# Eight gate tiles as four Strassen pairs, with a rearranged head, LayerNorm and last product, in a decoder layer

## The chip, the cores and the metric

The kernel runs on one NeuronCore of a Trainium2 chip. The metric is the device time of one execution in microseconds (us). Before the change the median of three runs is 1666.04 us (1663.42 to 1666.61).

## The reference

One step of a one-layer decoder over 16 meta tokens, 1024 prompt tokens and 8 samples of 8 new tokens, all in fp32:

```
u = rmsnorm(h);  z = u @ w_in + b_in            # 1024 -> 6144 columns
a, c, q, k, v, g = split(z)                     # g: three gates of 1024 channels
y_a = causal pooling of a, linear map           # branch A
y_b = GLU(c) -> depthwise conv, width 31 -> LayerNorm -> silu -> w_co   # branch B
y_c = attention(q, k, v) @ w_ao                 # branch C
h  += (sig(g0)*y_a + sig(g1)*y_b + sig(g2)*y_c) @ w_out
h  += relu(rmsnorm(h) @ w_up)**2 @ w_down
y   = rmsnorm(h)
```

The prompt's attention looks back 128 positions; the samples attend to a cache. The states of pooling, convolution and attention are outputs too.

## The kernel before

Activations lie with channels on the 128 partitions and tokens along the row: T = 1104 with the meta tokens, L = 1088 without. Every fp32 product is made of three fp32r products: a value is split into a high half (a rounding copy on ScalarE) and a low half (the value minus the high half, on DVE), and `mm3` (line 145) adds hi·hi, hi·lo and lo·hi in PSUM. So each weight tile costs a DMA, a ScalarE copy and a DVE subtraction ahead of its matmuls; `Weights` (line 45) does this: `split_to` emits the copy, and the subtraction is queued later, by `flush` or, one or two chunks on, by `tick`.

The input projection (lines 1042 to 1134) is 48 tiles of 128 output channels in the order of `TILES` (line 28), each in three token chunks `CH` of 416, 320 and 368 columns (400 instead of 416 where meta tokens aren't needed), with 24 matmuls a chunk. The first five tiles are the head (lines 1042 to 1115): there the norm isn't known yet, so raw x times the norm's weight is multiplied (`head_split`), and `head_stats` (line 341) makes the squares, their sums over channels (a matmul against ones, line 242), the reciprocal root on DVE and ScalarE, and a broadcast back by matmul (line 253); `rb` holds it, and `proj_chunk` scales by it. The last 13 tiles are gate tiles (kind "z"): `proj_chunk` (line 877) evicts each chunk on ScalarE with the bias (line 916) and stores it to a DRAM buffer `gD`.

Between chunks `slot` (line 207) runs one item of `attq` and some of `dveq`. `attq` holds attention: two items a unit (`even`: scores, transposes of the unit before, exponentials; `odd`: product with values, the next unit's split of q, normalization), then the samples, then loads and splits of the attention output `Ox` (`tail_slices`), then LayerNorm (`ln_steps`, put in by `after_conv` once `dveq` is empty). `dveq` holds the convolution's 31 taps of four channel groups and the pooling sums, two DVE instructions an item. An item of `attq` can say how many of `dveq` go with it: 1 in attention and in the samples' last six steps, none in their first eight; without one it is two (`NDVE`). Each engine works in the order in which its instructions are emitted.

Then come the attention output projection with the pooling product (lines 1155 to 1178, `pool_out`), the convolution's output projection (1190 to 1207), w_out (1321 to 1407), the up stage (1566 to 1632) and the down stage (1749 to 1809). The up stage takes two output tiles at a time by Strassen's identity in Winograd's form: weights A and activations B are cut into 2 x 2 blocks (two tiles by two halves of channels, two halves of channels by two halves of tokens), and seven products of sums of blocks, each of 24 matmuls of 272 columns, take the place of eight. `sum_pair` makes sums of weight blocks, `prep` splits a product's weights three products ahead, `product` multiplies. The down stage does the same over whole products, with sums that went through DRAM. Its last product (n = 6, lines 1780 to 1807) goes through the tokens in two parts; `residual` (line 1673) loads the saved h and adds it, through `page2`, a pool of five buffers.

Large buffers are 40 pages of T columns (`page`, line 124). PSUM has eight banks: three "pm" and two "qk" for main products (the "qk" ones are in the rotation only while `wide` is set), three "px" for the rest.

Of the kernel before, what the change touches and what calls it, by code (L numbers as in the profile page):

```python
# [7 lines left out]
F32 = mybir.dt.float32  # L8
# [27 lines left out]
NHEAD = 5  # L36
LAST_A = max(i for i, t in enumerate(TILES) if t[0] in "ac")
NDVE = (2, 2)
SMP = [0] * 8 + [1] * 6

# [4 lines left out]
class Weights:  # L45
# [10 lines left out]
    def load_to(self, n):  # L56
        while self.nraw < min(n, len(self.jobs)):
            i = self.nraw
            src, w, paged = self.jobs[i]
            t = self.tile("wraw", F32, w, paged)  # L60
            self.nc.sync.dma_start(t, src)
            self.raw[i] = t
            self.nraw += 1

    def load_half(self, i, h):
        src = self.jobs[i][0]
        if h == 0:
            self.raw[i] = self.tile("wraw", F32, 1024, False)
            self.nraw = i + 1
        c = slice(512 * h, 512 * h + 512)  # L70
        self.nc.sync.dma_start(self.raw[i][:, c], src[:, c])

    def split_half(self, i, h):
        if h == 0:
            self.out[i] = [self.tile(t, F32R, 1024, False) for t in ("whi", "wlo")]
            self.nsplit = i + 1
        c = slice(512 * h, 512 * h + 512)
# [4 lines left out]
    def split_to(self, n):  # L82
        while self.nsplit < min(n, len(self.jobs)):
            i = self.nsplit
            self.load_to(i + 1)
            _, w, paged = self.jobs[i]
# [25 lines left out]
def hybrid_trunk_kernel(ctx, tc, I, O):  # L112
# [46 lines left out]
    jobs = [(I["w_in"][i], 1024, 1 < i < NHEAD) for i in range(48)]  # L159
    WAO = [48, 49] + list(range(51, 57))  # L160
    WPOOL = 50
    jobs += [(I["w_ao"][m], 1024, False) for m in range(8)]
# [6 lines left out]
    W = Weights(nc, pool, page, jobs)  # L169


    one = pool.tile([P, 4], F32, name="one", tag="st", bufs=8)
# [4 lines left out]
    def load_x(ci, k0=0, k1=8):  # L177
# [3 lines left out]
        for k in range(k0, k1, n):  # L181
            m = min(n, k1 - k)
            t = page("x")[:, :m * w].rearrange("p (k c) -> p k c", k=m)
# [4 lines left out]
    vec = const("vec", [P, NV])  # L188
    W.load_half(0, 0)
    load_x(0, 0, 4)  # L190
    W.load_half(0, 1)
    load_x(0, 4, 8)
    bin_ = const("b_in", [P, 48])
    W.load_half(1, 0)
    W.load_half(1, 1)
# [145 lines left out]
    def head_stats():  # L341
        x = X[0]
        sq = [t[:, o:o + b0] for t in [page("acc") for _ in range(3)] for o in (0, 512)]
        acc, sq = sq[:2], sq[2:]
# [9 lines left out]
        def s1():  # L354
            for i in range(3, 8):
                q = sq[1 + i % 3] if i > 3 else acc[1]
                A.activation(q, x[i], AF.Square)
# [1584 lines left out]
```

## Time and profile before

| | |
|---|---|
| median of three runs | 1666.04 us (1663.42 to 1666.61) |
| the profiled execution | 1661.65 us |
| its span on the core | 1659.8 us |
| mean granted TensorE clock | 0.997 of full speed |
| matmuls | 11552 |

In the profile PE is TensorE's matmuls, PEld its weight loads, DVE VectorE, ACT ScalarE, POOL GpSimd, SP SyncE, whose queue issues nearly all DMAs. A timeline row is start (us from the span's start), duration, engine, line, operation, output tile <- input tiles, shapes and count, and in brackets the idle time of the engine just before and what ended it. A matmul's duration includes its way through the array, so the rate is read from start to start. Where a row stands for several instructions, the duration is theirs together.

### The profile page before, as it was taken

Reading aid. Unit: us, or ns where it says so; the run is one execution under the profiler, and the core shown is the slowest. Engines: PE = TensorE matmul, PEld = TensorE weight load, DVE = VectorE, ACT = ScalarE, POOL = GpSimd, SP = SyncE. Lnnn points to the kernel's source line nnn. Section 1 sums busy time; section 2 is a strip of 40 time slices with the busy share of each in tenths; the row PEclk is TensorE's granted clock in tenths of the full one; section 3 lists DMA queues with packets and bytes.
Section 4 is the critical chain, followed back from the end, with each engine's and each line's share of the span. In section 5 each row is a group of like instructions: output and inputs, shape, how many; then the busy total and the mean of one; then the engine's idle time right before and its main releaser. Section 6 shows DMA issues by size and latency. Waiting matters only on the chain.

```text
span 1659.8 us, 29142 instructions
## 1 busy us (share of the span) xinstructions
PE 1637.1 (99%) x11552; PEld 1612.9 (97%) x11552; DVE 1111.1 (67%) x1877; ACT 748.2 (45%) x1424; POOL 314.4 (19%) x258
## 2 busy tenths in 40 slices
PE   8999999999999999999999999999999999999987
PEld 7999999999999999999999999999999999999987
DVE  7786767867667576344474688888887844466665
ACT  6537667467674342364243443332233533333331
POOL 1010000000010002212102535555555200000000
PEclk9999999999999999999999999999999999999999
DMA  6051221221225263353243357777776855566633
GB/s 207 15 122 39 83 67 44 72 70 51 71 69 174 97 207 102 106 210 119 93 163 134 132 165 252 242 245 246 247 244 230 324 191 183 183 198 200 209 134 102
DMA packets 132349, 250.78 MB, mean 151 GB/s; under 512 B 33428, under 2 KB 64629, under 8 KB 132213
## 3 DMA queue, kind: packets, MB, share of 16 engines
q1 hardware_dynamic: 131796, 248.53, 45.4%
q8 instruction: 90, 1.47, 0.4%
q14 instruction: 47, 0.38, 0.1%
q10 hardware_dynamic: 416, 0.39, 0.1%
HBM read 168.52 MB, written 80.36 MB: 150 GB/s over the span
## 4 chain that ended last, share of the span: by engine, by line
PE 94%; DVE 2%; DMA 1%; issue 1%; ACT 1%; SPq 0%; DVEq 0%; ACTq 0%
PE pm L148 13%; PE pm L150 13%; PE pm L149 13%; PE m L1652 7%; PE m L1648 7%; PE m L1650 7%; PE m L1458 6%; PE m L1456 6%; PE m L1459 6%; PE pn L148 3%; PE pn L149 3%; PE pn L150 3%; PE px L622 2%; PE px L610 2%; PE qk L569 2%
## 5 line engine op out<-in xcount | busy, mean ns | idle before, releaser
L148 PE MATMUL pm<-uh,whi 128*128 128x320 f32 (+3 forms) x1008 | 338.0, 335 | 6.4 <-ACT uh L324 6.4
L149 PE MATMUL pm<-ul,whi 128*128 128x320 f32 (+3 forms) x1008 | 332.2, 330 | 1.1 <-DVE ul L325 1.0
L150 PE MATMUL pm<-uh,wlo 128*128 128x320 f32 (+3 forms) x1008 | 331.8, 329 | 0.0
L1652 PE MATMUL m<-oph,wlo 128*128 128x272 f32 (+2 forms) x896 | 259.3, 289 | 3.1 <-DVE wlo L91 3.1
L1648 PE MATMUL m<-oph,whi 128*128 128x272 f32 (+2 forms) x896 | 259.5, 290 | 1.2 <-ACT whi L90 1.2
L1650 PE MATMUL m<-opl,whi 128*128 128x272 f32 (+2 forms) x896 | 258.9, 289 | 0.0
L90 ACT ACTIVATE whi<-wraw 128x1024 fp32r<-128x1024 f32 (+1 forms) x127 | 130.1, 1026 | 223.1 <-PE m L1650 145.1
L91 DVE TENSOR_TENSOR wlo<-wraw,whi 128x1024 fp32r<-128x1024 f32 (+1 forms) x127 | 157.8, 1244 | 88.1 <-ACT whi L90 88.0
L148 PEld LDWEIGHTS pm<-uh,whi 128*128 128x128 f32 x1008 | 190.2, 189 | 7.7 <-ACT uh L324 6.4
L149 PEld LDWEIGHTS pm<-ul,whi 128*128 128x128 f32 x1008 | 190.3, 189 | 3.7 <-DVE ul L325 3.1
L150 PEld LDWEIGHTS pm<-uh,wlo 128*128 128x128 f32 x1008 | 190.1, 189 | 0.1
L1652 PEld LDWEIGHTS m<-oph,wlo 128*128 128x128 f32 x896 | 169.4, 189 | 3.6 <-DVE wlo L91 3.6
L1648 PEld LDWEIGHTS m<-oph,whi 128*128 128x128 f32 x896 | 169.7, 189 | 1.4 <-ACT whi L90 1.4
L1650 PEld LDWEIGHTS m<-opl,whi 128*128 128x128 f32 x896 | 169.6, 189 | 0.0
L444 DVE SCALAR_TENSOR_TENSOR y<-ext,vec,y 128x1024 f32<-128x1024 f32 x120 | 154.7, 1289 | 0.0
L1456 PE MATMUL m<-bch,wlo 128*128 128x272 f32 x448 | 129.1, 288 | 0.6 <-DVE cb L1599 0.6
L1456 PE MATMUL m<-bch,whi 128*128 128x272 f32 x448 | 129.1, 288 | 0.2 <-ACT s L1591 0.2
L1459 PE MATMUL m<-bch,whi 128*128 128x272 f32 x448 | 129.1, 288 | 0.0
L1459 PE MATMUL m<-bch,wlo 128*128 128x272 f32 x448 | 129.1, 288 | 0.0
L1458 PE MATMUL m<-bcl,whi 128*128 128x272 f32 x448 | 129.0, 288 | 0.0
L1458 PE MATMUL m<-bcl,wlo 128*128 128x272 f32 x448 | 129.0, 288 | 0.0
L558 POOL TENSOR_TENSOR uq<-q,uq 128x128 fp32r<-128x128 f32 x64 | 34.7, 564 | 391.9 <-ACT uq L557 391.9
(373 smaller groups left out, 3725.2 us busy)
## 6 DMA issues: line engine op xcount, KB each, us to landing
wraw<-w_in SPq DMA_DIRECT2D x46, 512.0 KB, 3.8
opT<-d SPq DMA_DIRECT2D x64, 272.0 KB, 3.2
ld<-opT SPq DMA_DIRECT2D x32, 544.0 KB, 4.7
wd<-w_down SPq DMA_DIRECT2D x32, 512.0 KB, 6.2
sumD<-wd SPq DMA_DIRECT2D x32, 512.0 KB, 4.9
wraw<-sumD SPq DMA_DIRECT2D x32, 512.0 KB, 3.6
gt<-gD SPq DMA_DIRECT2D x24, 544.0 KB, 4.6
ld<-opB SPq DMA_DIRECT2D x23, 544.0 KB, 4.8
```

The source lines that it names most:

```text
L90: self.nc.scalar.activation(hi, r, AF.Copy)
L91: self.late.append(lambda lo=lo, r=r, hi=hi: self.nc.vector.tensor_tensor(lo, r, hi.bitcast(F32), ALU.subtract))
L148: PE.matmul(ps, lhsT=wh[k], rhs=xh, start=first and i == 0, stop=False)
L149: PE.matmul(ps, lhsT=wh[k], rhs=xl, start=False, stop=False)
L150: PE.matmul(ps, lhsT=wl[k], rhs=xh, start=False, stop=last and i == n - 1)
L444: V.scalar_tensor_tensor(y[:, :NP], e[:, k:k + NP], w, y[:, :NP], ALU.mult, ALU.add)
L1456: PE.matmul(ps, lhsT=wh, rhs=xh, start=first and k == 0, stop=False, skip_group_check=True)
L1458: PE.matmul(ps, lhsT=wh, rhs=xl, start=False, stop=False, skip_group_check=True)
L1459: PE.matmul(ps, lhsT=wl, rhs=xh, start=False, stop=k == 3, skip_group_check=True)
L1648: PE.matmul(ps, lhsT=wh[:, w], rhs=xh[:, r], start=k == 0, stop=False, skip_group_check=True)
L1650: PE.matmul(ps, lhsT=wh[:, w], rhs=xl[:, r], start=False, stop=False, skip_group_check=True)
L1652: PE.matmul(ps, lhsT=wl[:, w], rhs=xh[:, r], start=False, stop=k == 15, skip_group_check=True)
```

## The change

- **Gate tiles.** The plain loop ends after 40 tiles (`NZ`). The last eight, all gate tiles, are computed as four pairs with the up stage's seven products. Activations come from the split u: `z_sums` adds the halves back together and makes four sums, for each of four channel pairs, all on DVE, behind four chosen chunks of tiles 37 to 39; `z_split` splits the results T1 to T4. Tile 39 takes its chunks in the order 1, 2, 0. The attention buffers are given up before the first pair, and `page2` opens there. The first pair's sums of weights are made during and just behind tile 39, the next ones a pair ahead, on DVE.
- **Around them.** In attention's `odd` items two taps go instead of one; the last pooling group's steps go to the head of `dveq`. LayerNorm is queued after the pairs, in the attention output stage. `Ox` is loaded and split in the last pair. Sums of LayerNorm, the pooling product's add and the low half of q move from GpSimd to DVE.
- **Head.** The first loads are cut finer, x's first chunk has a layout of its own, `vec` is loaded by ScalarE's queue, 16 matmuls of zeros go ahead, all eight squares are made on ScalarE with seven adds on DVE. The matmuls that sum over tokens (hs[2]) now stand behind tile 2's first chunk, and tile 3's first chunk stands ahead of the broadcast (hs[3]).
- **Last product.** Residual loads are issued in products 3 to 5, in halves of `page2` buffers (`residual_load`); three weight tiles of the last product are loaded at the end of product 5, and two of its tiles are loaded into `page2`.

```diff
+NWARM = 16
+NZP = 4
+NZ = 48 - 2 * NZP
...
-    vec = const("vec", [P, NV])
-    W.load_half(0, 0)
-    load_x(0, 0, 4)
-    W.load_half(0, 1)
+    W.load_part(0, 0, 2)
+    load_x(0, 0, 2)
+    W.load_part(0, 2, 4)
+    load_x(0, 2, 4)
+    W.load_part(0, 4, 8)
     load_x(0, 4, 8)
...
     def head_stats():
...
-        def s0():
-            for i in range(3):
-                q = sq[0] if i else acc[0]
-                G.tensor_tensor(q, x[i], x[i], ALU.mult)
-                if i:
-                    G.tensor_tensor(acc[0], acc[0], q, ALU.add)
...
+        def s1(ks):
+            def go():
+                for i in ks:
+                    q = sq[i % 2] if i else acc
+                    A.activation(q, x[i], AF.Square)
+                    if i:
+                        V.tensor_tensor(acc, acc, q, ALU.add)
+            return go
...
-            G.tensor_tensor(acc[:, :L], Y[0][:, :L], Y[1][:, :L], ALU.add)
+            V.tensor_tensor(acc[:, :L], Y[0][:, :L], Y[1][:, :L], ALU.add)
...
-                G.tensor_tensor(self.ql[:, i], q, self.qh[:, i].bitcast(F32), ALU.subtract)
+                V.tensor_tensor(self.ql[:, i], q, self.qh[:, i].bitcast(F32), ALU.subtract)
...
-            out += [(even(n, not first), 1), (odd(n, not first), 1)]
+            out += [(even(n, not first), 1), (odd(n, not first), 2)]
...
+    def z_sums(k):
+        ua, ub = zt[k] = page("zu"), page("zu")
+        lo, hi = slice(0, HL), slice(HL, L)
+        for t, n in ((ua, k), (ub, k + 4)):
+            V.tensor_tensor(t[:, :L], Uh[n][:, NM:].bitcast(F32), Ul[n][:, NM:].bitcast(F32),
+                            ALU.add)
+        V.tensor_tensor(ua[:, lo], ua[:, hi], ua[:, lo], ALU.subtract)
+        V.tensor_tensor(ua[:, hi], ub[:, hi], ua[:, hi], ALU.subtract)
+        V.tensor_tensor(ub[:, hi], ub[:, hi], ua[:, lo], ALU.subtract)
+        V.tensor_tensor(ub[:, lo], ub[:, lo], ub[:, hi], ALU.subtract)
...
+    wz = paux()
+    for _ in range(NWARM):
+        PE.matmul(wz[:, :256], lhsT=warm[:, :P], rhs=warm[:, P:], start=True, stop=True)
...
-    hs[2]()
     proj_open(2)
     b0_.append(proj_mm(2, 0))
+    hs[2]()
     W.split_to(4)
     W.flush()
     for k in range(4, 8):
         head_split(1, k)
+    proj_open(3)
+    b0_.append(proj_mm(3, 0))
     hs[3]()
     W.split_to(5)
     W.flush()
...
-    proj_open(3)
-    b0_.append(proj_mm(3, 0))
     proj_chunk(1, 0, b0_[1])
...
+    ZS = [(NZ - 3, 2), (NZ - 2, 0), (NZ - 2, 2), (NZ - 1, 0)]
+    for ti in range(NHEAD, NZ):
         proj_open(ti)
         W.split_to(ti + 2)
+        if ti == NZ - 1:
+            load_pair(-NZP)
+        for n, ci in enumerate((0, 1, 2) if ti < NZ - 1 else (1, 2, 0)):
+            if ti == NZ - 1 and n:
+                sum_pair(-NZP, n - 1)
+            proj_chunk(ti, ci)
+            if (ti, n) in ZS:
+                z_sums(ZS.index((ti, n)))
+            if ti == NZ - 1 and n:
+                z_split("T2", 2 * n - 2)
+                z_split("T2", 2 * n - 1)
+                prep(-7 * NZP + n - 1)
+            slot(1, NDVE[0] if attq else NDVE[1])
+        proj_close(ti)
...
+    load_pair(1 - NZP)
+    for k in range(4):
+        z_split("T1", k)
+    prep(-7 * NZP + 2)
+    for n in (2, 3):
+        sum_pair(-NZP, n)
+    for x in ("T3", "T4"):
+        attq.extend(lambda x=x, k=k: [z_split(x, k), z_split(x, k + 1)] for k in (0, 2))
+    oq = [load_split(Ox, "o", oD[j]) for j in range(8)]
+    for s in range(-7 * NZP, 0):
+        j, i = divmod(s, 7)
...
+        if s + 3 < 0:
+            prep(s + 3)
+        if j < -1:
+            if 2 <= i < 6:
+                sum_pair(j + 1, i - 2)
...
+        product(b, s, i, i in (0, 1, 5), z_comb)
...
+        slot(1, 2)
+    dveq.append(after_conv)
+    wide.append(0)
...
-            G.tensor_tensor(pt[:, a:c], pt[:, a:c], g0[:, a:c], ALU.add)
+            V.tensor_tensor(pt[:, a:c], pt[:, a:c], g0[:, a:c], ALU.add)
...
+    def residual_load(m, half):
...
     def residual(m, half):
         a, c = half
-        t = page2("hr")
-        SP.dma_start(t[:, :HL], hD[m][:, a:c])
+        t = hr.pop((m, a))
...
+                if 3 <= n < 6 and hf:
+                    if n != 5:
+                        residual_load(2 * mp + (n == 3), HI)
+                    if n != 3:
+                        residual_load(2 * mp + (n == 5), LO)
+                if n == NPROD - 2 and q == 7:
+                    W.load_to(i + 4)
                 dprod(n, mp, hf, b, TWO)
                 WD.pop((n, mp, hf))
-                slot()
+                slot(3 if n == 4 and hf == 0 else 1)
```

## Rows read from the trace of the kernel before

**Rows 1.** The page's first part: busy time, share of the span, instructions.
```profile
PE 1637.1 (99%) x11552; PEld 1612.9 (97%) x11552; DVE 1111.1 (67%) x1877; ACT 748.2 (45%) x1424; POOL 314.4 (19%) x258
```

**Rows 2.** Waits of TensorE: line, who, us in total, times, longest.
```profile
PE m L1652 <- DVE wlo L91: 3.1, 2, 2.4
...
PE m L1648 <- ACT whi L90: 1.2, 1, 1.2
```

**Rows 3.** Timeline of ScalarE, 578 to 607 us: samples' last copy, evictions of chunk 2.
```profile
578.74 0.77 ACT L770 ACTIVATE os<-spv 64x256 f32<-64x256 f32 x2 [0.68 <-PE spv L765]
...
594.72 0.57 ACT L916 ACTIVATE zs<-pn,b_in 128x368 f32<-128x368 f32 x1 [3.49 <-PE pn L150]
...
606.56 0.57 ACT L916 ACTIVATE zs<-pm,b_in 128x368 f32<-128x368 f32 x1 [1.48 <-issue]
```

**Rows 4.** Timeline of ScalarE in the up stage: eviction of product 6, four pairs apart.
```profile
1005.18 0.62 ACT L1605 ACTIVATE cb<-m 128x544 f32<-128x544 f32 x1 [2.32 <-PE m L1459]
...
1089.26 0.62 ACT L1605 ACTIVATE cb<-m 128x544 f32<-128x544 f32 x1 [2.32 <-PE m L1459]
```

**Rows 5.** Timeline of DVE, 569 to 599 us.
```profile
569.01 1.23 DVE L91 TENSOR_TENSOR wlo<-wraw,whi 128x1024 fp32r<-128x1024 f32 x1 [4.86 <-ACT whi L90]
570.15 1.28 DVE L444 SCALAR_TENSOR_TENSOR y<-ext,vec,y 128x1024 f32<-128x1024 f32 x1
...
571.54 1.28 DVE L444 SCALAR_TENSOR_TENSOR y<-ext,vec,y 128x1024 f32<-128x1024 f32 x1
...
584.41 1.23 DVE L91 TENSOR_TENSOR wlo<-wraw,whi 128x1024 fp32r<-128x1024 f32 x1 [7.22 <-ACT whi L90]
...
596.32 2.50 DVE L154 TENSOR_TENSOR ol<-ld,oh 128x1088 fp32r<-128x1088 f32 x2 [7.89 <-ACT oh L153]
```

**Rows 6.** Timeline of DVE, 949 to 952 us: sums and splits of 544 columns.
```profile
949.01 0.72 DVE L1363 TENSOR_TENSOR t<-u 128x544 f32<-128x544 f32 x1
...
950.45 1.36 DVE L154 TENSOR_TENSOR bcl<-t,bch 128x544 fp32r<-128x544 f32 x2 [0.72 <-ACT bch L153]
```

**Rows 7.** Windows: length; busy PE, PEld, DVE, ACT, POOL; PEclk, DMA share, GB/s.
```profile
1599.60:1602.00 2.40, 0.08 (x1) 0.09 (x1) 2.37 (x4) 0.00 (x0) 0.00 (x0) 0.99 0.01 3
1602.00:1605.40 3.40, 3.40 (x14) 3.40 (x15) 1.85 (x7) 2.15 (x3) 0.00 (x0) 0.50 0.51 154
```

**Rows 8.** Timelines of the head: two rows of ScalarE, four of DVE, two of TensorE.
```profile
8.62 2.27 ACT L324 ACTIVATE uh<-x,vec 128x416 fp32r<-128x416 f32 x4
...
26.24 0.52 ACT L371 ACTIVATE rb<-px 128x416 f32<-128x416 f32 x1 [1.08 <-PE px L253]
...
12.29 2.32 DVE L325 SCALAR_TENSOR_TENSOR ul<-x,vec,uh 128x416 fp32r<-128x416 f32 x4
...
22.00 0.16 DVE L228 TENSOR_SCALAR st<-st 128x4 f32<-128x4 f32 x1
...
24.03 1.22 DVE L91 TENSOR_TENSOR wlo<-wraw,whi 128x1024 fp32r<-128x1024 f32 x1
...
27.74 1.23 DVE L91 TENSOR_TENSOR wlo<-wraw,whi 128x1024 fp32r<-128x1024 f32 x1 [0.64 <-ACT whi L90]
...
19.72 0.95 PE L242 MATMUL st<-ones,acc 128*128 128x1 f32 x8
...
34.95 0.72 PE L242 MATMUL st<-ones,sq 128*128 128x1 f32 x6
```

**Rows 9.** Timelines of the last product: DVE and TensorE.
```profile
1598.60 0.73 DVE L1678 TENSOR_TENSOR h<-h,hr 128x544 f32<-128x544 f32 x1 [5.56 <-DMA hr<-hD]
...
1601.92 0.60 PE L1652 MATMUL m<-oph,wlo 128*128 128x288 f32 x1 [2.37 <-DVE wlo L91]
```

**Rows 10.** Groups by form: a pooling product's eviction, busy us, mean ns, idle before.
```profile
L1150 DVE SCALAR_TENSOR_TENSOR gt<-pm,vec,gt 128x416 f32<-128x416 f32 x11 | 6.8, 647 | 0.6 <-ACT whi L90 0.4
```

**Rows 11.** Timelines of ScalarE and TensorE in attention, 142 to 147 us.
```profile
142.39 1.71 ACT L601 ACTIVATE lg<-lg,usm 128x256 f32<-128x256 f32 x4 [0.69 <-DVE usm L599]
...
145.52 1.09 PE L610 MATMUL px<-ident,lg 128*128 128x128 f32 x8
```

More of the change, by code (lines that the diff above doesn't have):

```diff
@@ L157, in hybrid_trunk_kernel @@
     ctx.enter_context(sched)
[L159 to L162, printed above, removed]
+    W = Weights(nc, pool, page, [(I["w_in"][i], 1024, 1 < i < NHEAD) for i in range(NZ)])
+    WAO = [0, 1] + list(range(3, 9))
+    WPOOL = 2
+    jobs = [(I["w_ao"][m], 1024, False) for m in range(8)]
     jobs.insert(WPOOL, (I["w_pool"], 1024, True))
@@ L168, in hybrid_trunk_kernel @@
     jobs += [(I["w_out"][m], 1024, False) for m in MORD]
-    W = Weights(nc, pool, page, jobs)
+    vec = pool.tile([P, NV], F32, name="vec", tag="vec")
+    A.dma_start(vec, I["vec"])
     one = pool.tile([P, 4], F32, name="one", tag="st", bufs=8)
@@ L475, in fin @@
             store(rD[g], r[:, :L])
[L476 removed]
+        fs = [add(n, 1 << n) for n in range(g + 1)] + [fin]
+        if g == 3:
+            dveq[:0] = fs
+        else:
+            dveq.extend(fs)
     Sx = []
@@ new lines, in prep @@
+    def prep(s):
+        j, i = divmod(s, 7)
+        a, b = raws[j]
+        x = ORD[i]
+        if x[0] == "A":
+            src = {"A11": a[:, :512], "A12": a[:, 512:], "A22": b[:, 512:]}[x]
+        else:
+            n = int(x[1]) - 1
+            src = Ssum[j][n // 2][:, 512 * (n % 2):512 * (n % 2) + 512]
+        tag = ("whi", "wlo")[s % 2]
+        t = pool.tile([P, 1024], F32R, name=tag, tag=tag, bufs=2)
+        split(t[:, :512], t[:, 512:], src)
+        WX[s] = t
+        if i == 6:
+            raws.pop(j)
+            Ssum.pop(j)
@@ new lines, in product @@
+    def product(b, s, i, first, op):
+        t = WX.pop(s)
+        for ch in range(2):
+            for k in range(4):
+                wh, wl = (t[:, o + 128 * k:o + 128 * k + 128] for o in (0, 512))
+                xh, xl = op(BX[i], k, ch)
+                ps = b[ch][:, :HL // 2]
+                PE.matmul(ps, lhsT=wh, rhs=xh, start=first and k == 0, stop=False,
+                          skip_group_check=True)
+                PE.matmul(ps, lhsT=wh, rhs=xl, start=False, stop=False, skip_group_check=True)
+                PE.matmul(ps, lhsT=wl, rhs=xh, start=False, stop=k == 3,
+                          skip_group_check=True)
@@ new lines, in hybrid_trunk_kernel @@
+    print("left", len(attq), len(dveq))
+    while attq:
+        slot(1, 1)
+    slot(0)
+    apool_ctx.__exit__(None, None, None)
+    pool2 = ctx.enter_context(tc.tile_pool(name="sb2", bufs=1, reuse_waits="tile"))
+    load_pair(1 - NZP)
+    for k in range(4):
+        z_split("T1", k)
[5 more added lines that the diff above has]
+    oq = [load_split(Ox, "o", oD[j]) for j in range(8)]
@@ new lines, in hybrid_trunk_kernel @@
+        if i > 4:
+            store(gD[TILES[ti + i - 5][1]], c[:, :L])
+        if i == 4 and j < -2:
+            load_pair(j + 2)
+        if j == -1:
+            if i == 4:
+                W = Weights(nc, pool, page, jobs)
+                W.load_to(2)
+                W.split_to(1)
+                W.flush()
+            for n in ((), (), (0, 1), (2, 3), (), (4, 5), (6, 7))[i]:
+                oq[n][1]()
+            for n in ((0, 1, 2), (), (3, 4), (5, 6), (7,), (), ())[i]:
+                oq[n][0]()
```

274 lines of the change are left out of this document (152 added, 122 removed).

## The prediction

> **What bounds the kernel now.** I read the page first: TensorE is busy for 99% of the span [rows 1], so time is either taken out of the matmul stream or put into gaps of it. TensorE's own list of waits came next [rows 2]: the last down product waits 3.1 us for a DVE split and 1.2 us for a ScalarE one, and in the rest of the kernel it hardly waits. Then the stages: ScalarE's evictions of the gate tiles give their period, since TensorE never pauses there: one tile (72 matmuls of 400, 320 and 368 columns) takes 606.56 - 594.72 = 11.84 us [rows 3], 164 ns a matmul. The up stage already runs the same identity on pairs with 272 columns a matmul: (1089.26 - 1005.18) / 4 = 21.02 us a pair [rows 4], 168 matmuls of 125 ns. Last, DVE around the place of the change: a tap costs 571.54 - 570.15 = 1.39 us, and DVE sits idle for 7.22 us before 584.41 [rows 5]: there is some room, and the question is how much.
>
> Durations are from the profiled execution, 1661.65 us (span 1659.8), 4.4 us under the median of 1666.04. The sum is made against 1661.65 and carried over to the median.
>
> **1. Matmuls of the eight tiles.** Two plain tiles take 23.68 us, a pair 21.02: 2.66 us saved on each of four pairs, -10.7 us. The fixed cost of a matmul eats half of the eighth that the identity saves. Product order, accumulators and evictions are the up stage's, which leaves TensorE without a wait, so inside the pairs I cost evictions, copies and pair sums (0.64 us on DVE each) at nothing: some 10 us of DVE work lie beside 21 us of matmuls. The Trainium skill speaks against this step (TensorE: Matmul & The Clock Gate, Back-to-back issue gap): it gives a sustained 81 ns for 128 columns and 131 ns for 512. A straight line through these is an estimate of 100 ns for 272 and 112 ns for the mean of 363, and a pair would be 0.7 us longer than two tiles, +2.8 us in all. The rows of this kernel have 125 and 164 ns and decide for the gain.
>
> **2. DVE at the first pair.** All new sums are queued on DVE, in order, behind taps. The rows give their prices: a low half of a weight 1.14 us to the next start, a tap 1.39, two 1088-wide ones 2.50 [rows 5], a 544-wide one 1.36 - 0.72 = 0.64 [rows 6], taken for 512 too. One z_sums is 2.50 + 4 x 0.64 = 5.06 us. Up to the low half at 569.01 the queue is unchanged in number, and DVE waits for that one, so this is where I start. From it to the low half of the first product's weights stand 2 low halves (2.3), 11 taps (15.3; counted from the slots, two each once attention is done), 4 z_sums (20.2), one pair sum, two T2 splits and the split itself (2.6): 40.4 us, so 609.4. Tile 39 ends on TensorE at 606.4 [rows 3]. The second product multiplies T1: before its splits come 3 more taps, one sum, two T2 splits and a weight split (6.7 us), then four T1 splits of 0.64: the first is done at 616.8, the last at 618.7. After that 14 of the 24 matmuls remain, 1.75 us: the second product ends at 620.4 where 606.4 + 6.0 = 612.4 was due, 8.0 us late. A gap of this size halves the clock: after the 2.4 us gap in the last product it was granted 0.50 for 3.4 us [rows 7], and part of that falls after the wait, 0.6 us. So +8.6 us. Bounds: 6 (splits and sums at 0.6, clock kept) and 16 (third rival).
>
> **3. Head.** Smaller first loads, 16 dummy matmuls and the squares moved off GpSimd bring the first chunk forward: the last high half of x is made at about 10.9 now (the copies from 8.62 in [rows 8]), set by arrival, and the low halves cost 0.58 us each without GpSimd beside them (2.32 for four, [rows 8]), so the last one is ready at 11.0 instead of 14.6. The dummy matmuls I cost at nothing: they run while data is on its way, and the first chunk is paced by these splits. Then 1.2 us for the low halves of tile 1 and seven sums of squares of 0.6 us on DVE, and tile 2's low half is done at 18.2. Its chunk's remaining 22 matmuls (0.19 us, scaled between the two rates of step 1) end at 22.4. Now the sums over tokens come behind that chunk, 0.9 us (the row at 19.72 in [rows 8]), and tile 3's weights are split behind them: DVE's chain from 22.00 until the low half is done at 25.25 is 3.25 us [rows 8]. In the kernel before, a whole chunk of matmuls lies beside that chain; here TensorE stands still in it. Third matmul at 26.5, chunk done at 30.7, broadcast to 31.6. Tile 4's weights are split behind the copy of the broadcast: from 26.24 to 28.97, 2.73 us [rows 8], bare again. Third matmul at 34.3, chunk done at 38.3 against 34.95 [rows 8]: +3.4 us (1.5 if x comes earlier, 6 if the gaps halve the clock).
>
> **4. Last product.** DVE waits 5.56 us for a residual's DMA with a weight's low half queued behind it, and TensorE for 2.37 us [rows 9]. The change issues these loads a product or more ahead and puts two weight loads into other buffers. The gap goes, with it the half clock (3.4 us at 0.50, 1.7 us lost [rows 7]) and the 1.2 us wait for ScalarE with 0.7 for DVE behind it (3.1 - 2.4) [rows 2]. That is 6.0; I take -5.5 (-3 if the five shared pages make SyncE's loads wait).
>
> **5. Attention output stage.** LayerNorm moves here from the gate tiles, and its sums and the pool adds go to DVE. At m = 1 two pool products of 9 matmuls (1.5 us) lie between three parts of it; DVE has 3.9 us a part and 3.3 us a product (0.65 an eviction [rows 10], the adds 0.5), five banks are free, and TensorE waits for an eviction twice: +1.8 us (0 to 4).
>
> **6. Attention.** A second tap in every other slot fills idle DVE. The low halves of q go from GpSimd to DVE, ahead of the softmax's sums. Transposes start at 145.52, ScalarE's scaling ends at 144.1 [rows 11]: 1.4 us to spare against 0.5 us later; only at the three GLU gate tiles in attention, where ScalarE loads tables, is there none. +1.0 us (0 to 4). SyncE's moved loads (outputs of attention, gates) have 21 us of matmuls beside them: nothing.
>
> Sum: -10.7 + 8.6 + 3.4 - 5.5 + 1.8 + 1.0 = -1.4 us, so 1660.2 against the profiled execution and **1664.6** against the median.
>
> **Rivals.**
> - *DVE and the head keep up* (0.24). If DVE begins z_sums further ahead than I read, or the head's chain finds work, steps 2, 3, 5 and 6 cost 3 us together: 1666.0 - 10.7 - 5.5 + 3 = 1652.8. For it: 7.22 us of idle DVE [rows 5]. Against it: 50 us of DVE work before the last T1 split in the 37 us from 569.0 to 606.4.
> - *z_sums wait for pages* (0.20, slower). Their pages come from the pool that the samples' attention used. If the first two are ones that its last product reads, DVE, in order, cannot start at 571.5 but at 578.7, when that product's copy begins [rows 3]. Every microsecond from 571.5 on is one at the second product: 7.2 more, 1671.8. For it: many pages are live there. Against it: loads of pages in that place wait little now.
> - *Narrow matmuls give nothing* (0.04). At 141 ns each a pair takes as long as two tiles, and the change is slower by 9: 1675. Against it: the up stage's 125 ns over sixteen pairs.
> - The forecast (0.52; its own range 1658 to 1670).
>
> **Numbers.** Within 0.2% (3.3 us) is about what a measurement of this kernel can tell from no change. Faster: all of the first rival and 0.15 of the forecast, 0.39. Slower: 0.16 of the second, 0.09 of the forecast, 0.02 of the third, 0.27. Same: 0.34. The range runs from just under the first rival to the second, 1651.5 to 1672.
>
> **What would show it.** In the trace of after: pairs of 21.0 us; waits of TensorE for DVE at the first two products of the first pair (8 us, the longer one at the T1 splits); two gaps of about 3 us in the head, behind the sums and behind the broadcast, for weight splits; none at the last product. Wrong would be: no wait at the first pair, a head that ends its fifth chunk before 35 us, or waits of DVE for TensorE before the first z_sums.

## The result and the profile after

The changed kernel takes 1679.99 us (median of four runs, 1678.65 to 1681.52) where the kernel before, on the same chip, takes 1664.84: 1.0093 times as long, 95% interval 1.0080 to 1.0105. That is 15.2 us slower and above the range. The profiled execution took 1681.52 us (span 1679.7), 19.9 us of span more than that of before; the rest to 15.2 is that the profiled execution of before lay 3.2 under its median and this one 1.5 above.

The page's first part, against [rows 1]:

```profile
PE 1643.6 (98%) x11664; PEld 1613.1 (96%) x11664; DVE 1195.5 (71%) x2081; ACT 769.3 (46%) x1475; POOL 230.5 (14%) x153
```

The reader should see that TensorE's busy time rose by 6.5 us, though the identity takes 10.7 us of matmuls out. The clock explains most of that: at half clock a matmul of 416 columns starts every 0.35 us instead of every 0.19, and the stretches of low clock below, with one more between 1650 and 1656, come to 11.6 us of lost clock, against 1.7 before [rows 7]. So two views are needed, the waits and the granted clock. First TensorE's waits (line, who, us in total, times, longest), which before had one entry over 2 us besides the start [rows 2]:

```profile
PE zp L1121 <- DVE whi L160: 3.8, 1, 3.8
PE pm L154 <- DVE zc L1317: 2.8, 1, 2.8
PE zp L1120 <- DVE ul L160: 2.8, 1, 2.8
PE pn L154 <- ACT whi L96: 2.3, 2, 1.4
...
PE pm L154 <- ACT whi L96: 1.6, 1, 1.6
PE pn L156 <- DVE wlo L97: 1.4, 2, 0.8
...
PE pn L154 <- DVE gt L1351: 1.3, 1, 1.3
PE m L1118 <- DVE cb L1739: 1.1, 1, 1.1
PE pm L154 <- DVE gt L1351: 1.1, 1, 1.1
PE pm L154 <- DVE gt L1372: 1.1, 1, 1.1
```

Then windows laid around the stretches of low clock (length; busy PE with its matmuls; PEclk, DMA share, GB/s): head, first pair twice, start of the attention output stage, up stage.

```profile
26.50:33.70 7.20, 6.30 (x18) 0.53 0.02 8
33.70:35.50 1.80, 1.80 (x14) 1.00 0.00 0
622.40:627.00 4.60, 4.53 (x23) 0.65 0.32 132
629.70:634.50 4.80, 4.75 (x23) 0.64 0.00 0
716.00:720.00 4.00, 4.00 (x15) 0.58 0.82 281
1005.50:1009.20 3.70, 3.70 (x20) 0.58 0.61 236
```

In the first row 18 matmuls of 416 columns take 7.2 us, their waits included; in the second, at full clock, six of them take 1.2 us, and eight small ones of the broadcast follow. The lower level is 0.50, 1.2 of 2.4 GHz. Four of the five stretches stand right behind waits of the list; the last does not.

Laid stage by stage over before (times at which TensorE's stages start, from both timelines):

| start of | before | after | lag | grew by |
|---|---|---|---|---|
| tile 0, second chunk (head done) | 35.54 | 43.50 | 8.0 | 8.0 |
| tile 0, third chunk | 55.26 | 63.68 | 8.4 | 0.4 |
| the last eight tiles | 606.31 | 618.28 | 12.0 | 3.6 |
| attention output stage | 707.00 | 715.68 | 8.7 | -3.3 |
| convolution's projection | 814.45 | 834.79 | 20.3 | 11.7 |
| w_out | 862.14 | 882.41 | 20.3 | -0.1 |
| up stage | 957.85 | 978.60 | 20.8 | 0.5 |
| down stage | 1300.08 | 1323.75 | 23.7 | 2.9 |
| last matmul of the down stage ends | 1648.51 | 1667.90 | 19.4 | -4.3 |
| span | 1659.8 | 1679.7 | 19.9 | 0.5 |

LayerNorm's matmuls stood between the gate tiles before (the eight tiles took 100.7 us, where eight of 11.84 are 94.7) and stand in the attention output stage now: some 6.0 us changed stage there and belong to neither gain nor loss.

The pairs themselves run as predicted. ScalarE's last eviction of a pair, three pairs running:

```profile
649.81 0.49 ACT L1315 ACTIVATE zc<-zp,b_in 128x272 f32<-128x272 f32 x1 [1.01 <-PE zp L1121]
...
670.83 0.49 ACT L1315 ACTIVATE zc<-zp,b_in 128x272 f32<-128x272 f32 x1 [1.01 <-PE zp L1121]
...
691.86 0.49 ACT L1315 ACTIVATE zc<-zp,b_in 128x272 f32<-128x272 f32 x1 [1.01 <-PE zp L1121]
```

21.02 us a pair, the up stage's period [rows 4]; the first pair alone takes 31.3 us. The losses are around the pairs' own matmuls.

**Head.** Timeline of TensorE, ScalarE and DVE:

```profile
25.48 1.04 ACT L96 ACTIVATE whi<-wraw 128x1024 fp32r<-128x1024 f32 x1
26.57 0.72 PE L154 MATMUL pn<-uh,whi 128*128 128x416 f32 x1 [1.44 <-ACT whi L96]
27.19 1.22 DVE L97 TENSOR_TENSOR wlo<-wraw,whi 128x1024 fp32r<-128x1024 f32 x1
28.46 0.71 PE L156 MATMUL pn<-uh,wlo 128*128 128x416 f32 x1 [0.83 <-DVE wlo L97]
...
36.41 1.05 ACT L96 ACTIVATE whi<-wraw 128x1024 fp32r<-128x1024 f32 x1
37.51 0.45 PE L154 MATMUL pm<-uh,whi 128*128 128x400 f32 x1 [1.55 <-ACT whi L96]
```

Both bare gaps are where step 3 put them, tile 3's weights behind the sums and tile 4's behind the broadcast. The half clock begins in the first of them. A third gap, which step 3 did not have, stands ahead of them at tile 2's weights (0.9 and 0.6 us at 18.7 and 19.9).

**First pair.** DVE's first z_sums, the low half for the first product, the T1 splits, and TensorE's two waits:

```profile
583.52 2.49 DVE L1133 TENSOR_TENSOR zu<-uh,ul 128x1088 f32<-128x1088 f32 x2
...
621.72 0.69 DVE L160 TENSOR_TENSOR whi<-wraw,whi 128x512 fp32r<-128x512 f32 x1
622.46 0.39 PE L1121 MATMUL zp<-uh,whi 128*128 128x272 f32 x1 [3.77 <-DVE whi L160]
...
628.98 2.62 DVE L160 TENSOR_TENSOR ul<-zu,uh 128x544 fp32r<-128x544 f32 x4
629.75 0.39 PE L1120 MATMUL zp<-ul,wlo 128*128 128x272 f32 x1 [2.76 <-DVE ul L160]
```

From 582.13 to 634 no DVE row in this stretch has idle time ahead of it.

**Start of the attention output stage.** SyncE's loads of its first weights, and what follows:

```profile
706.31 0.81 SPq L67 DMA_DIRECT2D wraw<-w_ao  x2
...
712.81 1.06 ACT L96 ACTIVATE whi<-wraw 128x1024 fp32r<-128x1024 f32 x1 [6.37 <-PE zp L1120]
...
713.90 1.22 DVE L97 TENSOR_TENSOR wlo<-wraw,whi 128x1024 fp32r<-128x1024 f32 x1 [4.45 <-ACT whi L96]
715.04 0.90 DVE L1317 SCALAR_TENSOR_TENSOR zc<-zp,b_in,zc 128x272 f32<-128x272 f32 x2
...
715.68 0.46 PE L154 MATMUL pm<-oh,whi 128*128 128x416 f32 x1 [2.83 <-DVE zc L1317]
```

The two loads are issued at 706.3 and 706.7, behind loads of the attention output in SyncE's queue, of which one waits 3.2 us for a split on DVE; the first is copied 6.5 us after its issue, the second lands after 7.3. ScalarE's copy waits for it (the list names TensorE, which had passed that point), the low half waits on DVE for the copy, the eviction of product 5 stands behind the low half, and TensorE waits for the eviction's bank. The prediction had counted SyncE's moved loads as nothing. One theory is that the load needs a buffer which the last pair's weights hold; SyncE's own list of waits shows none for this load, so its place in the queue is a rival.

### The profile page after: what moved, and what is told of

Its sections match the earlier page's. It is cut to its first block, busy times and chain, and to the rows that moved or that the text cites. A ratio compares the mean times of both kernels' runs of the same rounds, so it can differ in the third digit from the quotient of the medians.

```text
span 1679.7 us, 29413 instructions
## 1 busy us (share of the span) xinstructions
PE 1643.6 (98%) x11664; PEld 1613.1 (96%) x11664; DVE 1195.5 (71%) x2081; ACT 769.3 (46%) x1475; POOL 230.5 (14%) x153
## 4 chain that ended last, share of the span: by engine, by line
PE 82%; DVE 11%; ACT 4%; DMA 2%; issue 1%; SPq 0%; DVEq 0%; ACTq 0%
PE pm L154 9%; PE pm L156 9%; PE pm L155 9%; PE m L1788 7%; PE m L1790 7%; PE m L1792 7%; PE m L1118 6%; PE m L1121 6%; PE m L1120 6%; PE pn L156 2%; PE pn L154 2%; PE pn L155 2%; DVE y L464 2%; PE zp L1120 2%; PE zp L1121 1%; PE zp L1118 1%
## 5 line engine op out<-in xcount | busy, mean ns | idle before, releaser
L154 PE MATMUL pm<-uh,whi 128*128 128x320 f32 (+3 forms) x912 | 304.8, 334 | 2.5 <-ACT whi L96 1.6
L155 PE MATMUL pm<-ul,whi 128*128 128x320 f32 (+3 forms) x912 | 299.6, 329 | 0.6 <-DVE ul L344 0.6
L156 PE MATMUL pm<-uh,wlo 128*128 128x320 f32 (+3 forms) x912 | 299.5, 328 | 0.6 <-DVE wlo L97 0.6
L97 DVE TENSOR_TENSOR wlo<-wraw,whi 128x1024 fp32r<-128x1024 f32 (+1 forms) x119 | 146.5, 1232 | 89.9 <-ACT whi L96 89.8
L96 ACT ACTIVATE whi<-wraw 128x1024 fp32r<-128x1024 f32 (+1 forms) x119 | 121.6, 1023 | 172.1 <-PE m L1790 132.5
L154 PEld LDWEIGHTS pm<-uh,whi 128*128 128x128 f32 x912 | 171.5, 188 | 4.6 <-ACT whi L96 1.7
L155 PEld LDWEIGHTS pm<-ul,whi 128*128 128x128 f32 x912 | 171.7, 188 | 2.2 <-DVE ul L344 1.8
L156 PEld LDWEIGHTS pm<-uh,wlo 128*128 128x128 f32 x912 | 171.5, 188 | 1.1 <-DVE wlo L97 1.0
L1118 PEld LDWEIGHTS m<-bch,whi 128*128 128x128 f32 x448 | 85.0, 190 | 1.8 <-ACT s L1733 1.0
```

The source lines that it names most:

```text
L96: self.nc.scalar.activation(hi, r, AF.Copy)
L97: self.late.append(lambda lo=lo, r=r, hi=hi: self.nc.vector.tensor_tensor(lo, r, hi.bitcast(F32), ALU.subtract))
L154: PE.matmul(ps, lhsT=wh[k], rhs=xh, start=first and i == 0, stop=False)
L155: PE.matmul(ps, lhsT=wh[k], rhs=xl, start=False, stop=False)
L156: PE.matmul(ps, lhsT=wl[k], rhs=xh, start=False, stop=last and i == n - 1)
L1118: PE.matmul(ps, lhsT=wh, rhs=xh, start=first and k == 0, stop=False, skip_group_check=True)
```

## The experiments

All times are medians against the kernel before on the same chip (1663.4 to 1664.4 us there). "Gain" is against after's 1679.99. The first four runs share a chip, and so do the next four, the four behind those and the last two; between such groups a difference under some 1 us says nothing, as their kernels before differ by that much.

**The head's order**

```diff
+    hs[2]()
     proj_open(2)
     b0_.append(proj_mm(2, 0))
-    hs[2]()
...
-    proj_open(3)
-    b0_.append(proj_mm(3, 0))
     hs[3]()
...
     proj_chunk(0, 0, b0_[0])
+    proj_open(3)
+    b0_.append(proj_mm(3, 0))
```

> The kernel after, with only the two blocks of the head put back where the kernel before has them: the sums over tokens ahead of tile 2's first chunk, the broadcast ahead of tile 3's first chunk. Dummy matmuls, finer loads and squares on ScalarE stay. Theory (the order bares DVE's chains, and the gaps bring the half clock, which costs more than the gaps): the fifth chunk ends near 33 us in place of 43.5, no half clock between 20 and 40 us, and the median falls by 9 to 11 us, to about 1670. Rival (the dummy matmuls or the later squares bring the low clock): half clock stays near 26 us, and less than 4 us come back.

Measured: 1670.71 us, ratio 1.0046 (1.0028 to 1.0064), a gain of 9.3. The window over the place (length; PE with its matmuls; PEclk, DMA share, GB/s):

```profile
18.00:36.00 18.00, 18.00 (x108) 1.00 0.49 172
```

No gap, full clock, and tile 0's second chunk starts at 34.59, 8.9 us sooner. The order costs all of it: gaps of 6.0 us (0.91 + 0.61 + 1.44 + 0.83 + 1.55 + 0.63) and some 3.0 of half clock (tile 3's 24 matmuls took 8.3 us from 26.57 on, 0.8 of it a wait, where 24 of 0.19 are 4.6). Dummy matmuls, finer loads and the squares are still there, and win 0.95 us over before by these two profiles. How much that is worth is not shown: the same head ends between 34.3 and 36.4 in the seven further profiles that have it, and before's head at 37.5 in the profile of the last product's part alone.

**Taps out of the last two plain tiles**

```diff
-            slot(1, NDVE[0] if attq else NDVE[1])
+            slot(1, 0 if ti > NZ - 3 else NDVE[0])
```

> The kernel after, with no convolution taps in the last two plain tiles (12 taps of 1.39 us go into the four pairs, where DVE is idle for over 2 us a product). Theory (DVE's queue is what is late at the first pair): both waits of the first pair go (3.8 and 2.8 us) and the half clock that follows them (about 4 us): 10 us, to about 1670; the pairs stay at 21.0 us. Rival (T1 is split in place and has to wait for tile 39's last reads, so the second wait stays): 4 to 5 us come back, 1675.

Measured: 1684.08 us, ratio 1.0122 (1.0100 to 1.0143), 4.1 worse than after. A miss that tells much:

```profile
649.94 0.91 DVE L1317 SCALAR_TENSOR_TENSOR zc<-zp,b_in,zc 128x272 f32<-128x272 f32 x2
650.59 0.57 PE L1118 MATMUL zp<-zb,whi 128*128 128x272 f32 x1 [9.43 <-DVE zc L1317]
```

The waits of 3.8 and 2.8 us shrank to 0.7 and 0.6, so the rival (T1 in place) falls. But the taps (11, not the 12 expected: the queue runs out) now stand in DVE's queue in the first pair, between splits and evictions, and TensorE waits 9.4 us there for one eviction. The queue was late by its length, and moving the work by one pair only moved the wait.

**First attention output weight loaded earlier**

```diff
-    jobs = [(I["w_ao"][m], 1024, False) for m in range(8)]
+    jobs = [(I["w_ao"][m], 1024, False, *([lambda n: page2(n)] if m == 0 else [])) for m in range(8)]
...
-            if i == 4:
+            if i == 0:
                 W = Weights(nc, pool, page, jobs)
+                W.load_to(1)
+            if i == 4:
                 W.load_to(2)
```

> The kernel after, with the first weight tile of the attention output product loaded seven products earlier, into a buffer of the second pool, instead of into a buffer that the last pair's weights hold until they are split. Theory (ScalarE's copy of that tile waits for a late load, its low half stands in DVE's queue ahead of an eviction, and TensorE waits for the bank): the 2.8 us wait at the start of that stage goes, and with it the half clock of some 2 us: 4 to 5 us, to about 1675.5. Rival (DVE is late there with splits of the attention output, whatever the load does): less than 1 us.

Measured: 1676.36 us, ratio 1.0078 (1.0059 to 1.0096), a gain of 3.6. The load goes out at 693.71, four products earlier (the expectation's seven is a slip), and no longer stands behind the other loads; the run moved the buffer and the place in the queue together, and which of them counts is open. The copy now runs at 707.31, the 2.8 us wait is gone and the half clock with it; a wait of 1.0 us at the last pair's product 6 takes part of the place.

**The kernel before, with the last product's part alone**

```diff
     def residual(m, half):
         a, c = half
-        t = page2("hr")
-        SP.dma_start(t[:, :HL], hD[m][:, a:c])
+        t = hr.pop((m, a))
```

with the rest of that part of the change.

> The kernel before, with only the last product's part of the change: residual loads in products 3 to 5, three weight tiles ahead, two of them in other buffers. Theory (step 4 of the prediction stands by itself): waits of 2.4, 1.2 and 0.7 us and the half clock after the first go, 4 to 6 us, to about 1660. Rival (loads moved ahead collide with the operand loads of products 3 to 5): less than 2 us.

Measured: 1659.47 us, ratio 0.9976 (0.9967 to 0.9985), a gain of 4.0 over before (1663.42). No wait of the last product is left in its list, and the clock stays full there; its down stage takes 342.7 us against 348.4. So step 4's part stands alone, though of the 5.7 us in the down stage 4.0 reach the median; the end behind it is 0.8 us longer in this profile, with a new wait of 0.7 us for the final norm's sum. In the profile of after 1.7 us of the 6.0 were given back by a half clock between 1650 and 1656, behind that same wait. The wait alone does not decide it: of the fifteen profiles that have it, nine show a half clock there and six, this one among them, do not.

**Taps past the first pair**, on top of the head's order and the early load (by their own gains 1667.1 together)

```diff
-            slot(1, NDVE[0] if attq else NDVE[1])
+            slot(1, 0 if ti > NZ - 3 else NDVE[0])
...
-        slot(1, 2)
+        slot(1, 1 if j > -NZP else 0)
```

> The kernel after with the head's order and the early weight load of the two runs before (together about 1667 by their own gains), and with no taps in the last two plain tiles nor in the first pair, one behind each product of the other three pairs. Theory (the first pair is late only because DVE's queue is longer than the time up to it; moved past the first pair the taps find idle DVE): the waits of 3.8 and 2.8 us and the 9.4 us wait that the nearer placing brought are all gone, the four pairs take 84 to 86 us, and the median falls by 8 to 11 us to about 1658. Rival (splitting T1 in place waits for tile 39's reads): a wait of 3 us or more at the second product stays, 1662 or more.

Measured: 1658.32 us, ratio 0.9970 (0.9958 to 0.9981): 8.8 gained, faster than before. TensorE's waits:

```profile
...
PE pn L154 <- DVE gt L1353: 1.3, 1, 1.3
...
PE zp L1118 <- DVE zc L1317: 1.0, 1, 1.0
...
PE zp L1120 <- DVE ul L160: 0.6, 1, 0.6
```

None for the first pair is over 0.7, no half clock stands there, and from its first product to the next stage it is 87.6 us in place of 97.4 (95.5 in the next run, which has the early load and after's taps). The mechanism of step 2 is shown: 11 taps, 15.3 us of DVE at 1.39 each, were the backlog. Not all is back: the first pair takes 23.3 us where the next takes 21.0, as its second product, which needs the T1 splits, takes 5.1 us in place of 3.0.

**Low half of q on GpSimd**, on the same base

```diff
-                V.tensor_tensor(self.ql[:, i], q, self.qh[:, i].bitcast(F32), ALU.subtract)
+                G.tensor_tensor(self.ql[:, i], q, self.qh[:, i].bitcast(F32), ALU.subtract)
```

> The same two parts put right (about 1667), and only the low half of q put back on GpSimd; taps stay as in the kernel after. Theory (in attention the low half of q stands on DVE ahead of the softmax's sums, and the transposes wait): the 3.5 us that tiles 10 to 27 lose against the kernel before go, to about 1664. Rival (the second tap in every other slot is what delays the sums): less than 1 us comes back.

Measured: 1666.28 us, ratio 1.0018 (1.0009 to 1.0027), 0.8 under the base, which is a sum of gains and was not run, so the total shows nothing. The trace does: tiles 10 to 27 lose 1.9 us in place of 3.5, with a new wait of 0.8 us for GpSimd. Neither side is right alone.

**LayerNorm's sums on GpSimd**, on the same base

```diff
-                V.tensor_tensor(acc, sq[0], sq[1], ALU.add)
+                G.tensor_tensor(acc, sq[0], sq[1], ALU.add)
```

and so for the others of its sums.

> The same two parts put right (about 1667), and only LayerNorm's sums put back on GpSimd; the pooling product's adds stay on DVE. Theory (at m = 1 of the attention output stage three parts of LayerNorm and two pooling products meet on DVE): waits of 1.1, 1.3 and 1.1 us shrink to under 1 in sum, about 1665. Rival (GpSimd is slower and holds up the chain to the next part): the waits move to later parts of LayerNorm, no gain or a loss up to 2 us.

Measured: 1671.30 us, ratio 1.0048 (1.0033 to 1.0063), 4.2 worse than the base and 5.0 worse than the run before it; its attention output stage takes 121.1 us, that run's 117.7. The timelines of GpSimd and DVE at the start of the stage:

```profile
701.08 2.53 POOL L510 TENSOR_TENSOR lacc<-y 128x1088 f32<-128x1088 f32 x1 [211.68 <-DVE ol L160]
703.69 6.91 POOL L512 TENSOR_TENSOR lacc<-lacc,y 128x1088 f32<-128x1088 f32 x2
```

```profile
701.68 3.01 DVE L97 TENSOR_TENSOR wlo<-wraw,whi 128x1024 fp32r<-128x1024 f32 x1
...
705.44 2.80 DVE L160 TENSOR_TENSOR ol<-ld,oh 128x1088 fp32r<-128x1088 f32 x1
...
715.88 1.21 DVE L97 TENSOR_TENSOR wlo<-wraw,whi 128x1024 fp32r<-128x1024 f32 x1
```

GpSimd starts its adds 4.2 us ahead of the stage's first matmul, where DVE came to them 12.7 us behind it in the run before, and beside them DVE's subtractions take 3.01 and 2.80 us in place of 1.21 and 1.28. TensorE then waits 2.7 us for a split. The Trainium skill has this (GPSIMD Engine Reference, Specifications): GpSimd's way to SBUF is shared with VectorE and contends with DVE instructions of two SBUF inputs; these rows agree. Taking these sums off GpSimd was right.

**All five together**

> All of it together: head order, early weight load, taps past the first pair, low half of q and LayerNorm's sums on GpSimd. If the parts add up, 1667 less 9, 3 and 2, about 1653, under the kernel before with only the last product changed (1659.5). If each gain only uncovers the next wait, no better than 1659.

Measured: 1660.49 us, ratio 0.9980 (0.9971 to 0.9990): 2.2 worse than the taps alone, as LayerNorm's sums cost more than q's low half gives.

**The dummy matmuls' bank**, on top of the run with the taps

```diff
-    wz = paux()
+    wz = psum.tile([P, 512], F32, name="px", tag="pm", bufs=3)
```

> The kernel of the run with the taps past the first pair (1658.3), with the target of the 16 dummy matmuls taken from the banks of the main products instead of those for other uses. Theory (the dummy matmuls are the first to ask for a PSUM bank, so the three other banks come first in the address order, and the up stage's first product, on the first two banks, waits for the last eviction of w_out: 0.6 us, and a half clock of 3.4 us some 26 us later): that wait and that half clock go, 2 to 2.5 us, to about 1656. Rival (the wait comes from the count of main products, eight tiles fewer): no change, 0.6 us stays.

Measured: 1658.72 us, ratio 0.9969 (0.9957 to 0.9980), no gain. The wait of 0.6 us ahead of the up stage is gone (first product at 957.16, right behind w_out), as the bank theory wants, but the half clock at 984 us came all the same: that part of the theory falls. That the bank's address decides is argued; the run shows that the tag does.

**LayerNorm three slots later**, on top of that

```diff
-        return [s0, idle, idle, s2(0), s2(1), s2(2),
+        return [s0, idle, idle, idle, idle, idle, s2(0), s2(1), s2(2),
...
-        attq.extend(ln1 + [f for g in ln2 for f in (g, *[lambda: None] * 3)])
+        attq.extend(ln1 + [f for g in ln2 for f in (g, *[lambda: None] * 2)])
```

> The same with LayerNorm's three parts begun three slots later in the attention output stage, behind the two pooling products of m = 1. Theory (they meet there on DVE): the three waits of 1.1, 1.3 and 1.1 us go, 3 to 3.5 us, to about 1652.5. Rival (DVE is as busy two chunks later): the waits move, less than 1 us.

Measured: 1656.22 us, ratio 0.9955 (0.9940 to 0.9970), 2.5 gained. The stage takes 114.2 us in place of 117.6, and one wait of 0.8 us is left of three: DVE has room three slots later. (By their times in after only two of the three, at 746.39 and 748.81, stand at m = 1, where the expectation has all; the third is at 781.17.)

**No dummy matmuls**, on top of the run with the taps

```diff
-    for _ in range(NWARM):
-        PE.matmul(wz[:, :256], lhsT=warm[:, :P], rhs=warm[:, P:], start=True, stop=True)
```

> The run with the taps past the first pair (1658.3) without the 16 dummy matmuls. Theory: they are not needed, since the first chunk is paced by the splits of x, and the low clock of 8 to 12 us goes with them; the wait ahead of the up stage goes as well, because the main products are again the first to ask for a bank: 2 to 4 us in all, about 1655. Rival (they keep the clock up for the first chunk): the head gets 1 to 2 us longer, and the up stage's 2 us come back: about 1657.5.

Measured: 1657.61 us, ratio 0.9966 (0.9954 to 0.9978), 0.7 less than the run with the taps, measured on another chip: not clear of noise. The wait ahead of the up stage is gone. The head is 0.3 us longer, less than it varies between kernels with the same head (34.3 to 36.4). The low clock is not gone: without dummies the window of 8 to 12 us shows a granted clock of 1.00, but the matmuls themselves show the lower level up to 13.2 us, 0.35 us from start to start there and 0.19 behind:

```profile
12.47 0.55 PE L155 MATMUL pm<-ul,whi 128*128 128x416 f32 x1
12.81 0.55 PE L156 MATMUL pm<-uh,wlo 128*128 128x416 f32 x1
...
13.58 0.35 PE L156 MATMUL pm<-uh,wlo 128*128 128x416 f32 x1
13.77 0.35 PE L154 MATMUL pm<-uh,whi 128*128 128x416 f32 x1
```

With dummies the matmuls around 6 us run at the full level, and in six of eleven profiles a stretch of low clock follows between 8 and 17 us. So they do bring the clock up, as the rival says, but the first chunk is paced by the splits: no gain of theirs is shown, and step 3 had them at nothing.

**One tap in attention**, on top of LayerNorm later

```diff
-            out += [(even(n, not first), 1), (odd(n, not first), 2)]
+            out += [(even(n, not first), 1), (odd(n, not first), 1)]
...
-SMP = [0] * 8 + [1] * 6
+SMP = [1] * 14
...
-        slot(1, 1 if j > -NZP else 0)
+        slot(1, 2 if j > -NZP else 0)
```

> The run with LayerNorm later, with one tap instead of two behind attention's odd items, and the taps left over behind the samples' items and the products of the last three pairs, two each. Theory for attention (the second tap delays the softmax's sums): tiles 10 to 27 lose under 1.5 us against the kernel before, in place of 3.5. For the whole, DVE in the pairs should run over: 44 taps at 1.4 us are not to be had there, and LayerNorm starts late, 1655 to 1662. Rival (the low half of q alone is the cause): tiles 10 to 27 still lose 3 us or more.

Measured: 1656.23 us, ratio 0.9951 (0.9935 to 0.9968), the same as without it. Tiles 10 to 27 lose 0.7 us in place of 3.5, so one tap takes most of attention's loss away. ScalarE's waits for DVE in the softmax tell the two causes apart (us in total over attention):

| ScalarE waits ahead of | before | after | q's low half on GpSimd | one tap |
|---|---|---|---|---|
| the exponentials (for the maxima, usm) | 32.6 | 48.0 | 42.9 | 34.2 |
| the scaling (for the sums, usm) | 22.3 | 35.6 | 24.2 | 34.3 |

The second tap delays mainly the maxima ahead of the exponentials, the low half of q the sums ahead of the scaling. Their gains of 2.8 and 1.6 us are more than the 3.5 together: they overlap. The pairs take 90.1 us in place of 87.8, with three waits of 0.5 to 1.3 us for evictions, and the samples lose 0.9.

**Half of the second taps moved, and none**, both with LayerNorm later and without dummy matmuls

```diff
-            out += [(even(n, not first), 1), (odd(n, not first), 2)]
+            out += [(even(n, not first), 1), (odd(n, not first), 1 + n % 2)]
...
-        slot(1, 1 if j > -NZP else 0)
+        slot(1, 1 + (i % 3 == 0) if j > -NZP else 0)
```

> The run with LayerNorm later, without the dummy matmuls, and with the second tap only behind every other one of attention's odd items; the 16 taps left over go behind the products of the last three pairs, 10 a pair in place of 7. If the cost is one of density, tiles 10 to 27 lose about 1 us against the kernel before and the pairs stay under 88.5 us: 2 us or more better than the run beside it, about 1653. If each tap costs where it stands, half the loss leaves attention (1.7 us) and half comes back in the pairs (1.2 us): less than 1 us between the two.

> The run with LayerNorm later, without the dummy matmuls; taps as there, none moved out of attention. The gains of both add up if nothing new is uncovered: 1656.2 less 0.7, about 1655.5; attention loses 3.5 us as before, the four pairs take 87 us, and no wait of over 0.5 us stands between the third pair and the up stage but one of 0.8 in the attention output stage.

Measured: half moved, 1657.95 us, ratio 0.9966 (0.9954 to 0.9978); none moved, 1654.06 us, ratio 0.9945 (0.9932 to 0.9957). By the totals both readings fall: the first kernel wins 1.3 us in attention and loses 5.5 in the pairs (92.0 against 86.5 us). By the stages the second reading fits: 1.3 us of the loss stand in the third pair, with nine taps in place of five and a wait of 1.1 us for an eviction. The other 4.1 are in the fourth pair, where one tap is left: a wait of 2.6 us at the last product, for an eviction behind splits of the attention output, and a half clock behind it. The loads of those splits went out 1.1 us later than in the other kernel; why is open. So the price of a tap in the pairs is shown for the middle ones alone (in the run before, ten and eight taps cost 0.7 and 2.0 us). TensorE's waits of the second, the lowest median of all kernels here:

```profile
PE pm L154 <- ACT uh L341: 5.2, 2, 4.8
PE px L270 <- DVE diag L265: 1.7, 1, 1.7
PE px L1853 <- ACT fsq L1959: 1.3, 1, 1.3
PE m L1116 <- DVE cb L1736: 1.1, 1, 1.1
PE pn L154 <- DVE gt L1348: 0.8, 1, 0.8
```

By this list the start, the end and two short waits are left. By the starts of its stages there is more: attention's 3.5 us, 2.2 in the first pair, and a half clock in the up stage from 979.9 to 983.2.

## Why the prediction was wrong

By its steps, predicted against the stage table (spans of the profiled executions):

| step | predicted | measured | shown by |
|---|---|---|---|
| 1 matmuls of eight tiles | -10.7 | -10.7 | 21.02 us a pair |
| 2 DVE at the first pair | +8.6 | +10.3 | taps past the pair |
| 3 head | +3.4 | +8.4 | order put back |
| 4 last product | -5.5 | -4.3 | that part alone |
| 5 attention output stage | +1.8 | +8.7 | early load, LayerNorm later |
| 6 attention | +1.0 | +3.6 | one tap |
| up stage, end | 0 | +3.8 | in part (below) |

- **Step 1** was right to 0.1 us; the third rival is out, and so is the 2.8 us loss that the prediction estimated from the Trainium skill (TensorE: Matmul & The Clock Gate, Back-to-back issue gap). One remark in it is wrong, without weight in the sum: an eighth of 23.68 is 2.96 us and the pair saves 2.66, so the fixed cost eats a tenth of the eighth, not half.
- **Step 2** named the right queue and both waits. The low half for the first product came 4.1 us behind tile 39's end (predicted 3.0), the last T1 split 13.3 (12.3). What was mis-sized is the half clock, put at 0.6 us: it stood in both stretches behind the waits, some 1.6 + 1.7 us by the windows above (4.60 x 0.35, 4.80 x 0.36). The waits themselves come to the rest of the 10.3, 7.0 us against 8.0 predicted, so the two errors partly cancel. The second rival's late start is out: z_sums began at 583.52, 12.0 us later than the 571.5 of before, as late as TensorE itself.
- **Step 3** failed most in size. Two gaps came where they were put (2.3 and 2.2 us), but a third, 1.5 us at tile 2's weights, was not in it: their low half was done at 19.9, not 18.2, and the chunk at 24.2, not 22.4. Tile 3's chunk then ran at half clock, 3.0 us more: the fifth chunk ended at 42.9 against 38.3 predicted and 34.95 before [rows 8]. The bound "6 if the gaps halve the clock" was in the text and was the likelier end; it was also short, since 6.0 us of gaps and 3.0 us of half clock are 9.0, less the 0.95 of the earlier start.
- **Step 4**: mechanism and size right (5.7 us in the down stage of that part alone, 4.0 in the median); after itself lost 1.7 of it to a half clock.
- **Step 5** is the step that failed in kind, with the "nothing" for SyncE's moved loads (it stands in step 6). The loads named there leave out the stage's first weight, which now goes out late, behind loads of the attention output: 3.0 us at the start (from start to start; 2.8 in the list) and a half clock of 1.7 behind it. At m = 1 TensorE waited twice, as predicted, for 2.4 us in place of 1.8; a third wait of 1.1 came at 781.17. Some 0.5 us of the 8.7 are open. The rows:

```profile
746.39 0.38 PE L154 MATMUL pm<-rh,whi 128*128 128x256 f32 x1 [1.13 <-DVE gt L1351]
...
748.81 0.43 PE L154 MATMUL pn<-oh,whi 128*128 128x416 f32 x1 [1.25 <-DVE gt L1351]
```

- **Step 6** looked at q's low halves and called the second tap filling of idle time. Both cost: the tap delays the softmax's maxima, q's low halves its sums. Without the second tap 2.8 of the 3.5 us go, with q's low halves on GpSimd 1.6.
- **The up stage** was not in the sum. Of its 3.3 us, 0.6 is the dummy matmuls' bank, shown by two runs; 1.6 a half clock whose cause is open; the rest is two waits 0.5 and 0.6 us longer at its end, not tried.

The forecast's sign hung on small terms that each ignored either the clock or a queue. With head, first weight, taps and LayerNorm put right and the dummy matmuls out, 26 us come back, and the change that was 15 us slower becomes 10 us faster than before, some 5 us of them over the last product's part alone (1659.47 to 1654.06, on two chips). That is half of step 1. Most of the other half can be seen in the profile of that last run: attention still loses 3.5 us, and the pairs take 86.5 us in place of 84.1.

## What to carry to other kernels

Where TensorE never stops, price a new gap with the half clock that may follow: here it came behind gaps of 1.4, 3.8, 2.8 and 2.8 us and cost 1.6 to 3.0 us on top of each, while single gaps of 1.1 to 1.6 us elsewhere went without, and one of 0.7 us had it in nine profiles of fifteen. When an edit adds work to an in-order engine, look for where its queue is empty and place it there one item at a time; moved too near, 11 taps came back as a 9.4 us wait. And follow each moved load to its place in the queue and to the buffer that it needs: a weight load in the last pair went out late and cost 3.6 us with all that hung on it.

## What was not expected of the hardware

- TensorE's clock fell to half with no wait in front of it: just behind 1006 in after, 1.2 us behind the matmuls of one column that sum the norm over tokens (18 in a row, 1002.82 to 1004.85), in a stretch without a gap. Of the sixteen profiles of this study, all with these matmuls at this place, nine show it and seven, that of before among them, do not. What decides is open; it costs 1.6 us. With the place near 1650, which shows it in nine of fifteen, two profiles can differ by some 3 us without an edit having been seen to cause it.
- Beside GpSimd's adds of 1088 columns DVE's subtractions took 3.01 and 2.80 us in place of 1.21 and 1.28.
- The tag under which 16 matmuls of zeros took a PSUM bank at the start settled a wait of 0.6 us a thousand microseconds later (gone in the run that changes it and in the one without them); this is how the kernel's pool deals out banks, and the traces do not show which bank it was.
